# Four convolution blocks moved behind a residual norm with other row buffers, and 16 feed-forward blocks in the mixer

## The chip, the cores and the metric

The kernel runs on one core of a Trainium2 chip. The metric is the device time in microseconds. A core has a matrix engine (TensorE, PE in the profile; PEld are its weight loads), a vector engine (VectorE, DVE), an activation engine (ScalarE, ACT), GpSimd (POOL) and an engine that here only issues transfers (SyncE, SP). They run side by side, each through its own list of instructions in order, and wait for each other on semaphores.

## The reference

One layer over 1024 tokens of 1024 channels, float32. After an input norm, a combined projection feeds two groups of channels: 512 channels of RWKV-7 time mixing (a recurrence over tokens, 8 heads of 64) and 512 channels of a gated causal convolution with 31 taps, a layer norm and a silu. Both go through one output projection `w_out`, then a norm and a residual sum, then a gated feed-forward network whose inner activations pass a causal convolution of 3 taps.

```python
c = u[..., :D_CONV] * jax.nn.sigmoid(u[..., D_CONV:])
c = _causal_dwconv(c, cconv_w, cconv_b)          # 31 taps
c = jax.nn.silu(_layer_norm(c, cln_g, cln_b))
...
x1 = x + rms_norm(concat(rwkv_out, c) @ w_out)   # residual norm behind the mixer
f  = causal_conv3(rms_norm(x1) @ ffn_up)         # 2 x 2816 columns
out = x1 + rms_norm((gelu(f[:, :2816]) * f[:, 2816:]) @ ffn_down)
```

(The last three lines are shortened to what they compute.)

## The kernel before

The tokens are worked on in two halves of 512, and the recurrence in four quarters of 256 with four chunks of 64 tokens each. Every float32 matmul is made of three, with weights and activations split into a high and a low part: `wh` and `wl` of a weight (a cast on ScalarE, a subtraction on GpSimd, line 154), `f` and `h` pairs of activations.

The convolution of one half is four blocks of 128 channels, `conv(h, i)`. A block is one ScalarE instruction that starts an accumulator in the single PSUM bank "pc" and 30 VectorE instructions on it (line 393), the last of which writes the tile "co". `conv_norm(h)` then does the layer norm of the four blocks through transposes on TensorE, and its silu writes the tiles "co" again, which `w_out(h)` reads beside the recurrence's output "mixr".

`norm_ffn(0)` is the residual norm between the first half's w_out and its feed-forward part. For each of four row blocks of 128 tokens it loads x, loads two pieces of w_out's result from DRAM (`mixd`) into tiles "pt", adds them (line 838), squares the sum on ScalarE (line 839), and writes the row to DRAM (`x1d`). The rows are then scaled and transposed by TensorE with a diagonal matrix (line 846), and `channels` splits the result into the pairs "f" (lines 257 and 259), which are the input of the feed-forward blocks. Its last VectorE instruction is kept in `self.mark_lo`. The tiles "pt" are six, four of which hold results of the recurrence at that time.

A feed-forward block (`ffn_pair`) has two products of 24 matmuls with 512 columns; ScalarE starts the sum from the bank "pb", of which there are two (line 863), VectorE adds two taps (line 868), ScalarE does the gelu and VectorE multiplies the two (line 875). Of the first half's 22 blocks the mixer holds EARLY; their results stay in row tiles for the first KEPT, and the others go to DRAM as `early` and are read back when the feed-forward phase begins, after `w_out(1)`.

The order is made when the kernel is built. A list scheduler takes, for each engine, the ready instruction of the best stream: first, the recurrence ("rwkv", 1000), "top" (the first half's residual norm), "norm", "conv", "proj" (projections and feed-forward blocks), a smaller number being better; weight splits and the copies out of banks go ahead of their stream. With `issue_after` a step is not placed before a named instruction. `W[3].mark` is the last step of the inverses of quarter 3; `sts[0]["normed"]` is the last silu of `conv_norm(0)`.

Of the kernel before, what the change touches and what calls it, by code (L numbers as in the profile page):

```python
# [16 lines left out]
AF = mybir.ActivationFunctionType  # L17
ALU = mybir.AluOpType
# [4 lines left out]
P = 128  # L23
# [3 lines left out]
HALF = 512  # L27
# [19 lines left out]
BUFS = {"v": 2, "gd": 1, "pt": 6, "kk": 1, "l8": 5, "ca": 6, "ck": 6, "r": 2,  # L47
        "mixr": 1, "co": 4, "po": 1, "c": 4, "t2": 2}

EARLY, KEPT, EVERY = 12, 8, 2  # L50

PRIO = {"first": -1000, "top": 100000, "rwkv": 1000, "norm": 200000, "conv": 300000, "proj": 400000}

# [25 lines left out]
def constants():  # L79
    c = np.zeros((P, NCONST), np.float32)  # L80

    def put(name, v):
        c[:, COFF[name][0]:COFF[name][1]] = v

    i = np.arange(P)
    put("ident", np.eye(P))
    put("blk", (i[:, None] // 64) == (i[None, :] // 64))
    put("mask", (i[:, None] % CH) <= np.arange(-1, CH)[None, :])
    put("scan", (np.arange(QUARTER) % CH != 0)[None, :])
    return c  # L90


class Trunk:
# [714 lines left out]
    def row(self, tag, n):  # L808
        return (self.rowp if tag == "row" else self.nrowp).tile([P, D], F32, tag=tag, bufs=n, name=self.nm(tag))

    def norm_ffn(self, h, row, piece, hs, ahead=2, tags=("pn",), dg=None):


        nc = self.nc
        rows, diags = [], []
        cut = lambda c: slice(c * 512, (c + 1) * 512)

        def channels(tp):
            if not tp:
                hs.extend(self.pairs("f"))  # L820
            ts = slice(2 * tp, 2 * tp + 2)
            self.channels(rows[ts], "pre_ffn", hs, slice(tp * 256, (tp + 1) * 256), tags, diags[ts] or None)

        r = self.small.tile([P, 8], F32, tag="nr", bufs=1, name=self.nm("nr"))
        sf = self.small.tile([P, 4, 4], F32, tag="sf", bufs=1, name=self.nm("sf"))
        nc.vector.tensor_reduce(r[:, 0:4], self.ssq[:, 4 * h:4 * h + 4], AX.X, ALU.add)
        self.rstd(r[:, 4:8], r[:, 0:4], 1.0 / D, RMS_EPS)
        for t in range(4):
            if t == ahead:
                channels(0)  # L830
            tt = 4 * h + t
            rs = slice(tt * P, (tt + 1) * P)
            x, s = row(), sf[:, t]
            nc.sync.dma_start(x, self.a["x"][rs])
            for c in range(2):
                m = piece()
                nc.sync.dma_start(m, self.mixd[rs, cut(c)])
                nc.vector.scalar_tensor_tensor(x[:, cut(c)], m, r[:, 4 + t:5 + t], x[:, cut(c)], ALU.mult, ALU.add)
                nc.scalar.activation(m, x[:, cut(c)], AF.Square, accum_out=s[:, c:c + 1])
            nc.sync.dma_start(self.x1d[rs], x)  # L840
            nc.vector.tensor_tensor(s[:, 2:3], s[:, 0:1], s[:, 1:2], ALU.add)
            self.rstd(s[:, 3:4], s[:, 2:3], 1.0 / D, RMS_EPS)
            if dg is None:
                nc.scalar.activation(x, x, AF.Copy, scale=s[:, 3:4])
            else:
                nc.vector.tensor_scalar(dg[:, t], self.con("ident"), s[:, 3:4], None, ALU.mult)
                diags.append(dg[:, t])
            rows.append((x[:, :512], x[:, 512:]))
            yield
        channels(1)  # L850

# [101 lines left out]
    def run(self):  # L953
        self.setup()
        sts = [{}, {}]
        with ExitStack() as ctx:
            self.setup_mixer(ctx)
            h0, early = self.mixer(sts)
        with ExitStack() as ctx:
            self.setup_ffn(ctx)  # L960
            h1 = []
            norm = self.norm_ffn(1, lambda: self.row("nrow", 4),
                                 lambda: self.f2p.tile([P, HALF], F32, tag="f2", name=self.nm("m")), h1, 3)
            acts = self.ffn_up(0, h0, islice(norm, 3), EVERY, early)
            list(norm)
            outs = []
            self.ffn_down(0, acts, lambda *a: outs.append(a))
            acts = self.ffn_up(1, h1, (self.ffn_out(*a) for a in outs), 2)
            self.ffn_down(1, acts, self.ffn_out)

    def mixer(self, sts):
        nc, tc = self.nc, self.tc
        W = [None] * 4
# [32 lines left out]
        def step(fn, q, *args):  # L1006
            if q < 4:
                with self.stream("rwkv"):
                    fn(W[q], *args)
# [31 lines left out]
        def conv(h, i, behind=None):  # L1041

            with ExitStack() as gate, self.stream("conv"):
                if behind is not None:
                    gate.enter_context(tc.issue_after(behind.ins))
                self.conv(sts[h], i)
# [9 lines left out]
        cut = lambda t: (t[:, :512], t[:, 512:])  # L1056
        with self.stream("norm"):
            two = [self.tl("l8", [P, 2, D]) for _ in range(2)]
            rows = [cut(two[t // 2][:, t % 2]) for t in range(4)]
# [10 lines left out]
        with self.stream("norm"):  # L1070
            two = self.tl("mixr", [P, 2, D])
            rows = [cut(two[:, t]) for t in range(2)]
# [21 lines left out]
        prepare(2)  # L1094
        project(1, hs, "v0 v1 g")
        step(self.bonus, 2)
        conv(1, 0, sts[0]["normed"])
        conv(1, 1, sts[0]["normed"])
        with self.stream("proj"):
            self.w_out(0, mixes[0], [sts[0]["co", i] for i in range(4)])  # L1100
        mixes[1] = self.tl("mixr", [P, 4, HALF])
# [1 line left out]
        with self.stream("top"):  # L1103
            h0 = []
            dg = self.tl("kk", [P, 4, QUARTER]).rearrange("p a (b t) -> p (a b) t", b=2)
            list(self.norm_ffn(0, lambda: self.row("row", 4), lambda: self.tl("pt", [P, HALF]), h0, 2,
                               ("pb",), dg))
        conv(1, 2, W[3].mark)
        conv(1, 3)
        conv_norm(1)  # L1110
        early = []
# [16 lines left out]
def pack(ins):  # L1128
# [33 lines left out]
    def pad(v):  # L1162
# [15 lines left out]
    out["params"] = np.ascontiguousarray(  # L1178
        np.concatenate([vals[n].reshape(c, P) for n, c in PARAMS]).T)
    out["consts"] = constants()  # L1180
    out["post_mix"] = f("norm_post_mix")
    out["post_ffn"] = f("norm_post_ffn")
# [16 lines left out]
```

## Time and profile before

| | us |
|---|---|
| three runs, median | 1335.6 |
| lowest and highest | 1334.03, 1339.08 |
| profiled execution, own time | 1338.86 |
| its span | 1336.9 |
| TensorE busy | 1287.3 |
| VectorE busy | 761.1 |
| ScalarE busy | 668.1 |
| GpSimd busy | 574.6 |

Times inside the program are microseconds from the start of the span. In the groups of instructions, a line has the code line, the engine, the operation, what it writes and reads, the shapes and the count, then the busy time and the mean of one in ns, and behind the bar the idle time of the engine ahead of them with what ended it. In a table by stretch the columns are named in its head; PEclk is the clock granted to TensorE, 1.00 being 2.4 GHz. The busy time of a group of matmuls counts overlaps of groups twice.

### The profile page before, as it was taken

Reading aid. Unit: us, or ns where it says so; the run is one execution under the profiler, and the core shown is the slowest. Engines: PE = TensorE matmul, PEld = TensorE weight load, DVE = VectorE, ACT = ScalarE, POOL = GpSimd, SP = SyncE. Lnnn points to the kernel's source line nnn. Section 1 sums busy time; section 2 is a strip of 40 time slices with the busy share of each in tenths; the row PEclk is TensorE's granted clock in tenths of the full one; section 3 lists DMA queues with packets and bytes.
Section 4 is the critical chain, followed back from the end, with each engine's and each line's share of the span. In section 5 each row is a group of like instructions: output and inputs, shape, how many; then the busy total and the mean of one; then the engine's idle time right before and its main releaser. Section 6 shows DMA issues by size and latency. Waiting matters only on the chain.

```text
span 1336.9 us, 22830 instructions
## 1 busy us (share of the span) xinstructions
PE 1287.3 (96%) x8712; PEld 1044.5 (78%) x8712; DVE 761.1 (57%) x1342; ACT 668.1 (50%) x1324; POOL 574.6 (43%) x496
## 2 busy tenths in 40 slices
PE   6999989999899889999999999999999999999997
PEld 5777767777679867787799888888888888888886
DVE  5377998997799979894521645400046644441002
ACT  6563654657745764657543655522244444442222
POOL 4443423344333422454462545444454544454453
PEclk9999989999999999999999999999999999999999
DMA  6322211121123441222354543533334533333333
GB/s 213 82 75 62 73 40 49 49 72 54 50 68 103 136 158 42 72 61 82 103 161 142 189 142 111 181 95 95 95 111 143 154 106 95 98 100 95 95 95 111
DMA packets 73405, 135.60 MB, mean 101 GB/s; under 512 B 7920, under 2 KB 14448, under 8 KB 73296
## 3 DMA queue, kind: packets, MB, share of 16 engines
q1 hardware_dynamic: 73296, 134.14, 33.6%
q8 instruction: 69, 1.13, 0.4%
q14 instruction: 40, 0.33, 0.1%
HBM read 120.48 MB, written 13.63 MB: 100 GB/s over the span
## 4 chain that ended last, share of the span: by engine, by line
PE 78%; DVE 13%; ACT 4%; issue 3%; POOL 1%; DMA 1%; SPq 0%; POOLq 0%; DVEq 0%; ACTq 0%
PE pb L127 68%; PE pe L127 4%; DVE pc L393 4%; PE xs L127 3%; POOL wl L154 1%; DVE dw L570 1%; PE pe L142 1%; DVE sub L568 1%; ACT wh L154 1%; DVE h L259 1%; DVE pt L462 1%; DMA pt<-mixd 0%; DVE kk L463 0%; DVE m L154 0%; PE pc L142 0%
## 5 line engine op out<-in xcount | busy, mean ns | idle before, releaser
L154 POOL TENSOR_TENSOR wl<-wr,wh 128x512 fp32r<-128x512 f32 x360 | 474.8, 1320 | 600.2 <-ACT wh L154 573.2
L127 PE MATMUL pb<-f,wh 128*128 128x512 f32 x1408 | 438.4, 392 | 2.4 <-ACT pb L765 1.8
L154 ACT CAST wh<-wr 128x512 fp32r<-128x512 f32 x360 | 221.5, 616 | 431.3 <-PE pb L127 251.1
L127 PEld LDWEIGHTS pb<-f,wh 128*128 128x128 f32 x1408 | 264.0, 189 | 57.8 <-ACT pb L765 2.0
L127 PE MATMUL pb<-f,wl 128*128 128x512 f32 x704 | 277.2, 394 | 0.9 <-POOL wl L154 0.9
L127 PE MATMUL pb<-h,wh 128*128 128x512 f32 (+3 forms) x720 | 230.4, 400 | 2.0 <-ACT wh L154 1.4
L393 DVE SCALAR_TENSOR_TENSOR pc<-c,params,pc 128x512 f32<-128x512 f32 x232 | 174.1, 750 | 4.6 <-ACT pc L390 0.5
L868 DVE SCALAR_TENSOR_TENSOR acc<-pb,params,acc 128x511 f32<-128x511 f32 (+1 forms) x128 | 95.5, 746 | 138.7 <-ACT acc L863 98.0
L127 PEld LDWEIGHTS pb<-h,wh 128*128 128x128 f32 (+2 forms) x720 | 132.4, 189 | 34.3 <-ACT wh L154 3.4
L127 PEld LDWEIGHTS pb<-f,wl 128*128 128x128 f32 x704 | 132.7, 188 | 30.6 <-POOL wl L154 2.9
L127 PE MATMUL pb<-h,wl 128*128 128x512 f32 (+3 forms) x360 | 146.8, 408 | 2.8 <-POOL wl L154 2.7
L927 DVE TENSOR_TENSOR row<-pb,post_ffn 128x512 f32<-128x512 f32 x16 | 10.2, 685 | 209.2 <-ACT junk L926 209.2
L127 PE MATMUL pb<-wl,ahi 128*128 128x512 f32 x320 | 126.6, 396 | 0.0
L127 PE MATMUL pb<-wh,alo 128*128 128x512 f32 x320 | 126.4, 395 | 0.0
L127 PE MATMUL pb<-wh,ahi 128*128 128x512 f32 x320 | 88.5, 396 | 0.0
L127 PEld LDWEIGHTS pb<-h,wl 128*128 128x128 f32 (+2 forms) x360 | 67.9, 189 | 22.1 <-POOL wl L154 5.3
L127 PEld LDWEIGHTS pb<-wl,ahi 128*128 128x128 f32 x320 | 60.1, 188 | 14.6
L127 PEld LDWEIGHTS pb<-wh,alo 128*128 128x128 f32 x320 | 60.1, 188 | 14.4
L127 PEld LDWEIGHTS pb<-wh,ahi 128*128 128x128 f32 x320 | 59.7, 188 | 14.5
L868 DVE SCALAR_TENSOR_TENSOR pt<-pb,params,pt 128x511 f32<-128x511 f32 (+1 forms) x48 | 35.8, 745 | 33.5 <-ACT ecarry L865 33.1
L863 ACT ACTIVATE acc<-pb,params 128x512 f32<-128x512 f32 x64 | 49.6, 775 | 0.0
L154 DVE TENSOR_TENSOR alo<-acc,ahi 128x512 fp32r<-128x512 f32 x36 | 33.8, 945 | 22.2 <-ACT ahi L154 22.2
(268 smaller groups left out, 1785.7 us busy)
## 6 DMA issues: line engine op xcount, KB each, us to landing
wr<-ffn_up SPq DMA_DIRECT2D x176, 256.0 KB, 2.6
wr<-ffn_down SPq DMA_DIRECT2D x88, 256.0 KB, 2.6
wr<-w_in SPq DMA_DIRECT2D x80, 256.0 KB, 2.6
wr<-w_out SPq DMA_DIRECT2D x32, 256.0 KB, 2.7
mixd<-t SPq DMA_DIRECT2D x16, 256.0 KB, 3.4
nrow<-x1d SPq DMA_DIRECT2D x8, 512.0 KB, 4.2
out<-nrow SPq DMA_DIRECT2D x16, 256.0 KB, 2.4
l<-x SPq DMA_DIRECT2D x8, 256.0 KB, 5.6
```

The costliest lines, as they stand in the source:

```text
L127: return self.nc.tensor.matmul(out, lhsT, rhs, start=start, stop=stop, skip_group_check=skip)
L142: self.nc.tensor.transpose(out, in_, self.con("ident")[:n, :n])
L154: return self.nc.scalar.copy(hi, src), eng.tensor_tensor(lo, src, hi.bitcast(F32), ALU.subtract)
L259: self.mark_lo = nc.vector.scalar_tensor_tensor(lo[:, toks], pv, g, hi[:, toks].bitcast(F32), ALU.mult, ALU.subtract)
L393: nc.vector.scalar_tensor_tensor(out, c[:, j:j + HALF], w(j), acc, ALU.mult, ALU.add)
L462: nc.vector.tensor_tensor_scan(sg[:, l], self.con("scan"), sg[:, l], 0.0, ALU.mult, ALU.add)
L568: nc.vector.tensor_tensor(tv, dv[:, j + 1:, j:j + 1].broadcast_to([P, n, j]), dv[:, j:j + 1, :j].broadcast_to([P, n, j]), ALU.mult)
L570: nc.vector.tensor_tensor(dv[:, j + 1:, :j], dv[:, j + 1:, :j], tv, ALU.add)
L863: nc.scalar.activation(acc, ps, AF.Identity, scale=w(2), bias=self.par("fb", ch))
L868: nc.vector.scalar_tensor_tensor(acc[:, o:], ps[:, :HALF - o], w(j), acc[:, o:], ALU.mult, ALU.add)
L927: nc.vector.tensor_tensor(f[:, cs], ps, self.post_ffn[:, cs], ALU.mult)
```

## The change

All four blocks of the second half's convolution are built after `norm_ffn(0)`; the first is issued after `self.mark_lo`, and the others follow it through the bank "pc". Before, the first two were issued after `conv_norm(0)` and the other two after `W[3].mark`. The four row blocks of `norm_ffn(0)` live in two "row" tiles, a pair of "co" tiles and a pair of "t2" tiles, where they had four "row" tiles; x is loaded and x1d written in halves of 256 KB, in the second half's norm too. EARLY is 16 in place of 12, so eight blocks go through DRAM where four did.

```diff
-EARLY, KEPT, EVERY = 12, 8, 2
+EARLY, KEPT, EVERY = 16, 8, 2
+def cut2(t):
+    return t[:, :512], t[:, 512:]
...
-            nc.sync.dma_start(x, self.a["x"][rs])
+            for c in range(2):
+                nc.sync.dma_start(x[c], self.a["x"][rs, cut(c)])
             for c in range(2):
                 m = piece()
                 nc.sync.dma_start(m, self.mixd[rs, cut(c)])
-                nc.vector.scalar_tensor_tensor(x[:, cut(c)], m, r[:, 4 + t:5 + t], x[:, cut(c)], ALU.mult, ALU.add)
-                nc.scalar.activation(m, x[:, cut(c)], AF.Square, accum_out=s[:, c:c + 1])
-            nc.sync.dma_start(self.x1d[rs], x)
+                nc.vector.scalar_tensor_tensor(x[c], m, r[:, 4 + t:5 + t], x[c], ALU.mult, ALU.add)
+                nc.scalar.activation(m, x[c], AF.Square, accum_out=s[:, c:c + 1])
+                nc.sync.dma_start(self.x1d[rs, cut(c)], x[c])
...
-                nc.scalar.activation(x, x, AF.Copy, scale=s[:, 3:4])
+                for c in range(2):
+                    nc.scalar.activation(x[c], x[c], AF.Copy, scale=s[:, 3:4])
...
-        conv(1, 0, sts[0]["normed"])
-        conv(1, 1, sts[0]["normed"])
         with self.stream("proj"):
             self.w_out(0, mixes[0], [sts[0]["co", i] for i in range(4)])
...
-            list(self.norm_ffn(0, lambda: self.row("row", 4), lambda: self.tl("pt", [P, HALF]), h0, 2,
-                               ("pb",), dg))
-        conv(1, 2, W[3].mark)
+            homes = iter(['row', 'row', 'co', 't2'])
+
+            def row():
+                n = next(homes)
+                return cut2(self.row(n, 4)) if n == "row" else tuple(self.tl(n, [P, HALF]) for _ in range(2))
+
+            list(self.norm_ffn(0, row, lambda: self.tl("pt", [P, HALF]), h0, 2, ("pb",), dg))
+        conv(1, 0, self.mark_lo)
+        conv(1, 1)
+        conv(1, 2)
         conv(1, 3)
         conv_norm(1)
```

The change moves lines: line 393 of the kernel before is line 397 after, 568 and 570 are 572 and 574, 868 is 874, 875 is 881, 890 is 896, 834 is 839, 838 is 843.

VectorE in the inverses of quarter 2 (`sub` and `dw`), before: the first convolution block of the second half (line 393) stands between their steps.

```order
448 L568 TENSOR_TENSOR sub_3965<-dw 128x14
449 L393 SCALAR_TENSOR_TENSOR pc_4564<-c_3301,params,pc_4564 128x512
450 L570 TENSOR_TENSOR dw<-dw,sub_3965 128x14
451 L393 SCALAR_TENSOR_TENSOR pc_4564<-c_3301,params,pc_4564 128x512
452 L568 TENSOR_TENSOR sub_3968<-dw 128x26
453 L723 TENSOR_TENSOR mixr_1958<-mixr_1958,gn_3898 128x4x128
454 L393 SCALAR_TENSOR_TENSOR pc_4564<-c_3301,params,pc_4564 128x512
455 L570 TENSOR_TENSOR dw<-dw,sub_3968 128x13x2
456 L393 SCALAR_TENSOR_TENSOR pc_4564<-c_3301,params,pc_4564 128x512
457 L568 TENSOR_TENSOR sub_3971<-dw 128x36
```

The same place after:

```order
448 L572 TENSOR_TENSOR sub_3971<-dw 128x36
449 L727 TENSOR_TENSOR mixr_1958<-mixr_1958,gn_3898 128x4x128
450 L574 TENSOR_TENSOR dw<-dw,sub_3971 128x12x3
451 L572 TENSOR_TENSOR sub_3974<-dw 128x44
452 L574 TENSOR_TENSOR dw<-dw,sub_3974 128x11x4
453 L572 TENSOR_TENSOR sub_3977<-dw 128x50
454 L574 TENSOR_TENSOR dw<-dw,sub_3977 128x10x5
455 L572 TENSOR_TENSOR sub_3980<-dw 128x54
```

The convolution steps are gone from between the steps of the inverse.

VectorE in the residual norm of the first half, before: the additions of the third and fourth row block (`row<-pt,nr,row`, line 838), the scores (`l` and `ca`, lines 517, 518 and 526) and the first splits `f` between them.

```order
599 L838 SCALAR_TENSOR_TENSOR row_5977<-pt_5983,nr_5887,row_5977 128x512
600 L517 TENSOR_TENSOR l_792_5254<-pe_5287,const 128x4x64
601 L518 TENSOR_TENSOR ca_5285<-pe_5287,const 128x4x64
602 L702 TENSOR_TENSOR r_5467<-xs_94,XG_5479 64x256
603 L838 SCALAR_TENSOR_TENSOR row_5993<-pt_5995,nr_5887,row_5993 128x512
604 L259 SCALAR_TENSOR_TENSOR f_5926<-pb_5941,params,f_5925 128x256
605 L259 SCALAR_TENSOR_TENSOR f_5928<-pb_5941,params,f_5927 128x256
606 L841 TENSOR_TENSOR sf_5888<-sf_5888 128x1
607 L526 TENSOR_TENSOR l_639_4014<-l_639_4014,gd_4235 128x1024
```

After, at the second and third row block (the third is in "co" tiles):

```order
580 L843 SCALAR_TENSOR_TENSOR row_5845<-pt_5853,nr_5821,row_5845 128x512
581 L574 TENSOR_TENSOR dw<-dw,sub_5374 128x5x10
582 L572 TENSOR_TENSOR sub_5377<-dw 128x44
583 L574 TENSOR_TENSOR dw<-dw,sub_5377 128x4x11
584 L846 TENSOR_TENSOR sf_5822<-sf_5822 128x1
585 L572 TENSOR_TENSOR sub_5380<-dw 128x36
586 L152 TENSOR_SCALAR var_5859<-sf_5822 128x1
587 L574 TENSOR_TENSOR dw<-dw,sub_5380 128x3x12
588 L572 TENSOR_TENSOR sub_5383<-dw 128x26
```

The scores have moved ahead of the norm, and steps of the inverses of quarter 3 stand between the additions.

SyncE where the feed-forward phase begins, before: the last pieces of w_out(1) are written, the blocks kept in DRAM come back, then rows of x and the first weights.

```order
231 L767 DMA mixd<-t_1214_8067 128x2x256
232 L890 DMA acc_8126<-early 128x512
233 L890 DMA acc_8132<-early 128x512
234 L890 DMA acc_8138<-early 128x512
235 L890 DMA acc_8144<-early 128x512
236 L834 DMA nrow_8336<-x 128x1024
237 L834 DMA nrow_8532<-x 128x1024
238 L834 DMA nrow_8728<-x 128x1024
239 L834 DMA nrow_9156<-x 128x1024
240 L160 DMA wr_8259<-ffn_up 128x512
```

After, the end of the same stretch:

```order
270 L164 DMA wr_8665<-ffn_up 128x512
271 L839 DMA nrow_9187<-x 128x512
272 L896 DMA acc_8520<-early 128x512
273 L896 DMA acc_8526<-early 128x512
274 L164 DMA wr_8683<-ffn_up 128x512
```

Six blocks come back ahead of these rows, and the last two stand between the weights.

## Rows read from the trace of the kernel before

**Rows 1.** The head of the page: the span, then the busy time, share and count of TensorE and its weight loads and of the other engines.

```profile
span 1336.9 us, 22830 instructions
...
PE 1287.3 (96%) x8712; PEld 1044.5 (78%) x8712; DVE 761.1 (57%) x1342; ACT 668.1 (50%) x1324; POOL 574.6 (43%) x496
```

**Rows 2.** The table by stretch: from and to, its length, busy time and count of PE, PEld, DVE, ACT and POOL, then the granted clock, the share of the DMA engines and GB/s.

```profile
368.60:397.50 28.90, 26.58 (x135) 20.97 (x134) 28.61 (x54) 13.48 (x25) 11.95 (x11) 0.96 0.25 71
397.50:463.60 66.10, 63.11 (x851) 58.59 (x849) 63.39 (x103) 42.81 (x97) 25.20 (x20) 0.99 0.37 107
463.60:510.20 46.60, 38.08 (x454) 28.64 (x453) 38.95 (x95) 29.27 (x77) 9.84 (x14) 0.90 0.42 134
510.20:626.00 115.80, 115.75 (x1150) 92.44 (x1151) 96.55 (x157) 66.05 (x139) 49.93 (x42) 0.99 0.23 65
...
727.60:732.00 4.40, 2.60 (x8) 1.91 (x7) 1.28 (x2) 2.67 (x9) 0.00 (x0) 0.77 0.42 135
732.00:861.00 129.00, 128.92 (x580) 106.08 (x579) 69.97 (x102) 73.38 (x149) 63.42 (x50) 0.99 0.49 156
```

**Rows 3.** The waits of TensorE: what waited, for whom, the time in total, how often, the longest. The first is of 368.6 to 397.5, the second of 397.5 to 463.6, the third of 463.6 to 510.2, the last two of 510.2 to 646.

```profile
PE pe L142 <- DVE mixr L737: 2.1, 1, 2.1
...
PE pb L127 <- POOL wl L154: 1.8, 2, 0.9
...
PE pb L127 <- DVE sub L568: 2.0, 1, 2.0
...
PE pc L142 <- DVE t L409: 1.3, 1, 1.3
PE pb L127 <- POOL wl L154: 0.6, 1, 0.6
```

**Rows 4.** Groups of VectorE from 368.6 to 463.6.

```profile
L393 DVE SCALAR_TENSOR_TENSOR pc<-c,params,pc 128x512 f32<-128x512 f32 x58 | 43.4, 748 | 0.6
```

**Rows 5.** Groups of TensorE's matmuls, the first three from 463.6 to 510.2 (scores, broadcasts of 512 columns, chunk products), the last from 510.2 to 626 (small steps of the inverses).

```profile
L127 PE MATMUL pe<-l,l 64*128 64x128 f32 x64 | 6.5, 290 | 0.9 <-DVE ca L518 0.6 <-DVE sf L841 0.4
L127 PE MATMUL pe<-pt,const 128*128 128x512 f32 x8 | 6.0, 866 | 0.1
L127 PE MATMUL Y<-r,l 64*64 64x64 f32 x48 | 4.6, 250 | 0.0
...
L127 PE MATMUL pe<-l,dw 32*16 32x16 f32 (+1 forms) x192 | 4.5, 178 | 0.0
```

**Rows 6.** The timeline of the gap: start, duration, engine, line, what was done, and in brackets the idle time ahead with what ended it. First VectorE (additions, the diagonal), then ScalarE (the last Square), then TensorE.

```profile
474.63 1.41 DVE L838 SCALAR_TENSOR_TENSOR row<-pt,nr,row 128x512 f32<-128x512 f32 x2
...
489.02 1.17 DVE L838 SCALAR_TENSOR_TENSOR row<-pt,nr,row 128x512 f32<-128x512 f32 x1
...
495.53 0.74 DVE L838 SCALAR_TENSOR_TENSOR row<-pt,nr,row 128x512 f32<-128x512 f32 x1
...
499.51 0.64 ACT L839 ACTIVATE pt<-row 128x512 f32<-128x512 f32 x1
...
507.14 1.42 PE L127 MATMUL pb<-kk,row 128*128 128x128 f32 x9 [2.02 <-DVE sub L568]
...
510.25 1.19 PE L127 MATMUL pb<-f,wh 128*128 128x512 f32 x2 [0.20 <-DVE sub L568]
```

**Rows 7.** The table by stretch again, where the granted clock falls; the columns as in rows 2.

```profile
463.60:467.10 3.50, 1.56 (x53) 1.25 (x53) 3.47 (x6) 2.82 (x10) 1.43 (x2) 1.00 0.87 183
...
467.10:473.90 6.80, 6.75 (x50) 3.51 (x49) 1.73 (x5) 3.05 (x10) 1.52 (x2) 0.50 0.85 274
508.10:511.50 3.40, 3.21 (x13) 2.74 (x12) 2.36 (x9) 1.68 (x4) 0.00 (x0) 0.50 0.01 2
```

**Rows 8.** Groups of VectorE beside the feed-forward blocks, the first three from 517.7 to 598.6 (convolution, gate, product), the others from 510.2 to 646 (group norm, low split).

```profile
L393 DVE SCALAR_TENSOR_TENSOR pc<-c,params,pc 128x512 f32<-128x512 f32 x58 | 43.6, 751 | 1.2 <-ACT pc L390 0.2
L868 DVE SCALAR_TENSOR_TENSOR pt<-pb,params,pt 128x511 f32<-128x511 f32 (+1 forms) x20 | 14.9, 743 | 1.6 <-ACT ecarry L865 1.6
L875 DVE TENSOR_TENSOR row<-pt,pt 128x512 f32<-128x512 f32 x5 | 4.5, 904 | 0.0
...
L723 DVE TENSOR_TENSOR mixr<-mixr,gn 128x512 f32<-128x512 f32 x4 | 5.7, 1424 | 0.3 <-POOL gn L149 0.3
L154 DVE TENSOR_TENSOR l<-mixr,l 128x512 fp32r<-128x512 f32 x4 | 4.2, 1118 | 4.2 <-ACT l L154 4.2
```

**Rows 9.** The timeline there: ScalarE takes up a product and VectorE ends it; then the end of the fourth convolution block and a product of the gate.

```profile
580.99 0.78 ACT L863 ACTIVATE pt<-pb,params 128x512 f32<-128x512 f32 x1
...
585.65 0.73 DVE L868 SCALAR_TENSOR_TENSOR pt<-pb,params,pt 128x510 f32<-128x510 f32 x1
...
591.81 0.73 DVE L393 SCALAR_TENSOR_TENSOR co<-c,params,pc 128x512 f32<-128x512 f32 x1
592.46 1.79 DVE L875 TENSOR_TENSOR row<-pt,pt 128x512 f32<-128x512 f32 x1
```

**Rows 10.** TensorE's timeline: the last transposes of the convolution's norm; the last feed-forward matmuls ahead of w_out(1), and its first.

```profile
642.82 0.63 PE L142 MATMUL pc<-const,t 128*128 128x128 f32 x4 [1.28 <-DVE t L409]
...
680.18 0.62 PE L127 MATMUL pb<-f,wh 128*128 128x512 f32 x2
...
681.55 1.12 PE L127 MATMUL pb<-wm,l 128*128 128x256 f32 x8
```

**Rows 11.** SyncE's timeline where the feed-forward phase begins.

```profile
730.73 1.76 SPq L890 DMA_DIRECT2D acc<-early  x4
```

More of the change, by code (lines that the diff above doesn't have):

```diff
@@ L847, in norm_ffn @@
                 diags.append(dg[:, t])
-            rows.append((x[:, :512], x[:, 512:]))
+            rows.append(x)
             yield
@@ L961, in run @@
             h1 = []
-            norm = self.norm_ffn(1, lambda: self.row("nrow", 4),
+            norm = self.norm_ffn(1, lambda: cut2(self.row("nrow", 4)),
                                  lambda: self.f2p.tile([P, HALF], F32, tag="f2", name=self.nm("m")), h1, 3)
```

## The prediction

> **What bounds the kernel now.** I read the head of the page first: TensorE is busy 1287.3 of the span's 1336.9 us [rows 1]. So an edit can only pay where TensorE stands still or runs at half clock, and I looked for those places with the table by stretch [rows 2]. From 732 us on nothing is left to win (128.92 of 129.00 us busy up to 861). Ahead of the first feed-forward matmul, at 510.25, three stretches lose something: the half's projections up to 397.5 (2.3 us idle, the difference of its length and its busy time), w_out of the first half (3.0 us) and the stretch from its end to 510.2, which I call the gap (8.5 us idle, at a granted clock of 0.90). The waits of TensorE say for whom [rows 3]: 2.1 us for VectorE's mixr, 1.8 us for weight splits of GpSimd, and in the gap many short ones. VectorE is the cause of the first: it is busy 28.61 of 28.90 and 63.39 of 66.10 us there [rows 2], and 58 instructions of the convolution at 748 ns, 43.4 us, are mixed into the chunk inverses [rows 4]. These are what the change takes away from there.
>
> **Part 1, projections and w_out(0).** The convolution steps leave VectorE between 368.6 and 463.6, so what else it does there ends up to 43 us earlier. The stretch up to 397.5 can give 2.3 us of idle time and 1.1 us that the clock of 0.96 costs in 28.9 us; most of it is the wait for mixr, which should go. I take 3 us (0 to 3.4), and w_out(0) starts at 394.5 in place of 397.5. In w_out(0) TensorE's order has 114 more matmuls than before (32 score products, 49 chunk products, two broadcasts of 512 columns, 31 small ones). Each stands for two records of the trace, so by the forms' rows [rows 5] a score is 0.20 us, a chunk product 0.19, a broadcast 1.5 and a small step 0.05: 6.5 + 9.3 + 3.0 + 1.6, some 20 us as groups; but the groups of the gap add up to 49 us where TensorE was busy 38, since matmuls overlap, and part of it ran at half clock. I take 14 us (12 to 17). That is work brought forward, no loss. Of the 3.0 us idle 2 go; the wait for weight splits stays. Gain 2, between 0 and 3. It ends at 394.5 + 66.1 + 14 - 2 = 472.6.
>
> **Part 2, the gap.** What sets its length is the chain of the residual norm, four row blocks one after the other [rows 6]. Only two "pt" tiles are free for the pieces of mixd, so each row block waits for a round trip: the first piece of row 1 is added at 474.63 and that of row 4 at 489.02, 4.8 us a row. To that come delays: the first addition stands behind a wait of VectorE for TensorE, 2.3 us after the norm's statistics were there; the last addition came at 495.53, some 5 us after its piece could have been used, behind other work on VectorE; its Square began at 499.51, 3.2 us after it, behind ScalarE's key copies; and TensorE waited 2.0 us for an inverse's step just before the first feed-forward matmul. These make 12.6 us, so the gap lies between 34 us (46.6 less all of them) and 46.6. In the new order the scores and key copies are over before the gap, but the inverses of quarter 3, 14 pairs of short steps, now stand between the additions, and two additions of "pt" that wait for TensorE stand behind the first pair. The round trip stays, since the change gives more row buffers and no more pieces. I take 40 us, the middle, and the first feed-forward matmul at 512.6. What the gap holds of TensorE's work falls: 32 scores, 49 chunk products and two broadcasts go, 160 small steps come; 18.8 us of groups against 8, and with the same overlap and clock some 5 to 9 us, I take 6. So of the 6.6 us by which the gap is shorter 6 were moved ahead: gain 0.6, between -5 and +7.
>
> The clock: after 1.56 busy of 3.50 us, from 463.6, the granted clock falls to 0.50, that is 1.2 GHz, and stays there to 473.9; at 508.1 it falls again [rows 7]. The Trainium skill says in "TensorE: Matmul & The Clock Gate", section "HAM oscillation — how this bites in real kernels", that waits between bursts of matmuls put the engine back to half clock, so that the next burst starts cold. The rows agree. A gap with less work in it would, by that rule, also lie at half clock at its end, which would add about 1 us to the first feed-forward block (3.4 us at half clock instead of the 1.25 us of it that lie behind 510.25); without the rule nothing changes in the sum.
>
> **Part 3, feed-forward beside convolution.** All 120 convolution steps now run from the first feed-forward block on, where 60 ran before. VectorE's order from there to the end of the fourth block: 120 x 751 ns = 90.1 us; 48 gate steps at 743 = 35.7; 12 products at 904 = 10.8; four each of the group norm and the lower split, 5.7 and 4.2 [rows 8]; 35 short ones, about 16. Sum 162 us. Neighbours that don't depend on each other start 0.08 us before the end of the one ahead (591.81 + 0.73 against 592.46 [rows 9]); some 150 such pairs make it 151 us. TensorE has 576 feed-forward matmuls until then, at 0.228 us each (six in 680.18 to 681.55 [rows 10]) 131 us, and 236 small ones, 17 to 25: 148 to 156 us. VectorE begins 3 us behind, with the first product, so at the end it is 2 behind (151 + 3 - 152). A product's bank was given back 5.4 us after ScalarE had taken it up (580.99 to 585.65 + 0.73 [rows 9]) in a stretch where TensorE stood still for 0.05 of 115.80 us [rows 2]. So no stop on balance: 0, between -1.9 (the waits of 1.3 us for the convolution's norm and of 0.6 for weights [rows 3] go too) and +14 (below).
>
> **Part 4, the rest.** Four more feed-forward blocks come before w_out(1) and four fewer after it: no change of TensorE's work. Between the norm of the convolution (its last transposes at 642.82) and w_out(1) (681.55 now [rows 10]) only 23 matmuls are left as cover, 5.2 us, where there were 38 us; a silu, the splits of "co" and the weights' casts must fit in: 0 to +3. After w_out(1) eight "early" blocks come back where four did; their four issues began at 730.73 [rows 11]. The last two reloads need a buffer that must first come free, and weights stand behind them on SyncE: 0 to +4. The stretch already loses 1.8 us of 4.4 [rows 2]. I take +0.5 for both. GpSimd's and ScalarE's work are the same in sum, and the rows written in halves, 256 KB, only let the first half land earlier: nothing.
>
> **Sum**, against the profiled execution's own 1338.86 us: -3 -2 -0.6 +0 +0.5 = -5.1, so 1333.8. That execution lies 3.3 us above the median of 1335.6. So 1330.5, I say 1330.
>
> **Rivals.** A: VectorE becomes the bound of the feed-forward stretch. Without the overlap of neighbours it needs 162 + 3 us against 148 of TensorE; less the 5.4 us of slack it stops TensorE for 12 us, and w_out(1) then also waits for the convolution's norm. It decides when VectorE really needs over about 155 us. For it: VectorE was busy 96.55 of 115.80 us [rows 2] with half of the steps; one product took 1.79 us (592.46 [rows 9]) where the five took 0.90 in the mean. Against it: before, it kept up with the same mix. The Trainium skill, "SBUF — State Buffer", section "SBUF: two separate sides", says that a VectorE instruction with two SBUF operands is held up by a GpSimd instruction that has the port pair they share. The trace agrees for the 1.79 us, while convolution steps, with one operand from PSUM, keep 751 ns beside busy GpSimd; by the rule the price falls on the 12 products and the splits alone, some 3 us. A gives 1330 + 12 = 1342, 1340 to 1346.
>
> B: the norm runs through at its round trips, 34 us, the rest of the idle time ahead goes (3.4 + 3.0 - 5 = 1.4 us) and so do the 1.9 us of waits in part 3: 6 + 1.4 + 1.9 better than the forecast, 1321. For it: scores and copies are out of its way. Against it: short inverse steps stand in every pair of additions.
>
> C: the idle time only moves. The chunk products fill w_out, the gap keeps 46.6 us and has less to fill it: 6.6 us back, 1337, no change. For it: the last wait ahead of the feed-forward blocks [rows 6] is for an inverse of the recurrence, not for the norm.
>
> **Chances.** Forecast 0.45 (its own range 1325 to 1336), A 0.20, B 0.20, C 0.15. The range 1319 to 1344 holds B's and most of A's. A difference under 0.5%, 6.7 us, can't be told from none: faster is below 1328.9, slower above 1342.3. B and four in ten of the forecast make faster 0.38; half of A and what I have not seen make slower 0.17; the same is 0.45.
>
> **What would show it.** The first matmul of w_out(0) near 394.5, its last near 473; the first feed-forward matmul near 513; between there and the end of the convolution no wait of TensorE for VectorE's gate steps. Long waits for a bank there mean A; a gap of 35 us B; one of 46 C. The forecast is wrong altogether if w_out(1) begins over 10 us after its last feed-forward matmul.

## The result and the profile after

The changed kernel takes 1340.2 us in the median of 19 executions (1337.0 to 1347.4), the kernel before 1335.8 us beside it. The ratio of the means is 1.0046, 95% interval 1.0028 to 1.0063: slower by some 6 us in the mean and 4.4 in the median, where a gain of 5 was forecast. The interval leaves no room for a gain.

The 19 times are no one heap. Ten lie at 1337.0 to 1340.2 and nine at 1342.8 to 1347.4. In all executions of the changed order in this study (this kernel, and three that differ from it in buffers or reloads only, 66 in all) none lies between 1340.3 and 1342.2: 40 are below, with a mean granted clock of 0.980 to 0.988, and 26 above, at 0.974 to 0.983 (18 of them under 0.980). I call them the lower and the upper group; their means here are 1338.3 and 1345.9 us. The profile below is of an execution of the lower group, 1337.5 us. That it is shorter than the profile of before (1338.9) is therefore no sign of a gain.

The table by stretch of the changed kernel, with the columns of [rows 2]. The first stretch ends at the first matmul of w_out(0), the second at its last, the third (the gap) at the first feed-forward matmul.

```profile
368.60:392.10 23.50, 21.57 (x113) 16.79 (x112) 20.76 (x46) 12.94 (x24) 10.30 (x10) 1.00 0.23 64
392.10:474.20 82.10, 79.56 (x1077) 71.61 (x1075) 47.78 (x78) 46.74 (x109) 26.08 (x24) 0.98 0.33 102
474.20:515.90 41.70, 31.65 (x575) 26.37 (x573) 30.97 (x81) 27.32 (x69) 7.74 (x12) 0.84 0.39 130
515.90:680.00 164.10, 163.33 (x1054) 130.91 (x1051) 152.84 (x226) 84.06 (x176) 75.23 (x59) 1.00 0.30 88
```

VectorE is no longer full ahead of w_out(0) and beside it (20.76 of 23.50 and 47.78 of 82.10 us, where [rows 2] have 28.61 of 28.90 and 63.39 of 66.10), as the change intends. It is nearly full beside the feed-forward blocks, 152.84 of 164.10, and TensorE doesn't suffer from that: 163.33 us busy. The gap is shorter, 41.7 for 46.6 us, at a clock of 0.84 for 0.90.

The waits of TensorE in the same kernel, as in [rows 3]: the first up to 392, the next three in the gap, the last two from 516 to 680.

```profile
PE pe L146 <- DVE mixr L727: 1.9, 1, 1.9
...
PE pb L131 <- DVE sf L846: 2.4, 1, 2.4
PE pe L131 <- issue: 1.7, 1, 1.7
PE xs L131 <- ACT r L696: 1.3, 1, 1.3
...
PE pb L131 <- DVE pt L874: 0.3, 1, 0.3
PE pb L131 <- POOL wl L158: 0.3, 1, 0.3
```

The wait for mixr that was to go with the convolution (2.1 us in [rows 3]) is still there with 1.9. For VectorE's gate steps TensorE waits 0.3 us in all.

The gap's timeline, as in [rows 6], and the end of the convolution's norm, as in [rows 10]:

```profile
481.58 1.21 DVE L843 SCALAR_TENSOR_TENSOR row<-pt,nr,row 128x512 f32<-128x512 f32 x1
...
498.80 0.74 DVE L843 SCALAR_TENSOR_TENSOR t<-pt,nr,t 128x512 f32<-128x512 f32 x1
...
502.18 0.75 DVE L843 SCALAR_TENSOR_TENSOR t<-pt,nr,t 128x512 f32<-128x512 f32 x1
...
515.90 0.73 PE L131 MATMUL pb<-f,wh 128*128 128x512 f32 x2
...
715.52 0.60 PE L146 MATMUL pc<-const,t 128*128 128x128 f32 x4
...
721.00 0.88 PE L131 MATMUL pb<-wm,l 128*128 128x256 f32 x6
```

The first piece of the fourth row block is added 17.2 us after that of the first (before 14.4), its second piece follows 3.4 us later (before 6.5). The last transposes of the norm come at 715.52, without a wait, and w_out(1) follows its last feed-forward matmul at 721.00.

### The profile page after: what moved, and what is told of

Its sections match the earlier page's. It is cut to its first block, busy times and chain, and to the rows that moved or that the text cites. A ratio compares the mean times of both kernels' runs of the same rounds, so it can differ in the third digit from the quotient of the medians.

```text
span 1335.4 us, 22890 instructions
## 1 busy us (share of the span) xinstructions
PE 1284.2 (96%) x8712; PEld 1044.5 (78%) x8712; DVE 763.5 (57%) x1342; ACT 669.9 (50%) x1330; POOL 574.3 (43%) x496
## 5 line engine op out<-in xcount | busy, mean ns | idle before, releaser
L874 DVE SCALAR_TENSOR_TENSOR acc<-pb,params,acc 128x511 f32<-128x511 f32 x112 | 83.4, 745 | 116.9 <-ACT acc L869 98.0
L933 DVE TENSOR_TENSOR row<-pb,post_ffn 128x512 f32<-128x512 f32 x16 | 10.2, 685 | 206.3 <-ACT junk L932 206.3
L131 PEld LDWEIGHTS pb<-wh,alo 128*128 128x128 f32 x320 | 60.1, 188 | 14.4
L874 DVE SCALAR_TENSOR_TENSOR pt<-pb,params,pt 128x511 f32<-128x511 f32 x64 | 47.7, 745 | 14.0 <-ACT ecarry L871 13.4
L869 ACT ACTIVATE acc<-pb,params 128x512 f32<-128x512 f32 x56 | 43.4, 774 | 0.0
```

The source lines that it names most:

```text
L131: return self.nc.tensor.matmul(out, lhsT, rhs, start=start, stop=stop, skip_group_check=skip)
L869: nc.scalar.activation(acc, ps, AF.Identity, scale=w(2), bias=self.par("fb", ch))
L874: nc.vector.scalar_tensor_tensor(acc[:, o:], ps[:, :HALF - o], w(j), acc[:, o:], ALU.mult, ALU.add)
L933: nc.vector.tensor_tensor(f[:, cs], ps, self.post_ffn[:, cs], ALU.mult)
```

## The experiments

**The same kernel again.** No edit.

> The changed kernel once more, for the spread of its times and another profile. Its runs lie in two groups, ten at 1337 to 1340 us and nine at 1343 to 1347, and the profile read so far (1337.5) is of the lower one. Theory K (clock): the upper group has TensorE at 1.2 GHz for some 16 us more, so its mean granted clock is near 0.977 where the lower has 0.980 to 0.988; this would be around or behind the gap between w_out(0) and the first feed-forward block, which holds less matmul work now. Theory E (early blocks): the upper group comes from the feed-forward phase's start, where eight blocks come back from DRAM, and the clock is only a sign of it. Both: median 1338 to 1344.

Measured: 1338.8 us median of 11 executions, ratio 1.0015 (1.0004 to 1.0026); eight in the lower group, three in the upper (1342.3 to 1344.6). The profile fell on the lowest of the upper, 1342.3 us. A later profile (the version with eight buffers, below) fell on 1347.2 us. Of that one, the table by stretch where the feed-forward blocks begin, at 523.3:

```profile
505.00:510.00 5.00, 4.23 (x135) 3.96 (x134) 3.29 (x11) 2.91 (x8) 1.10 (x2) 0.78 0.26 96
510.00:515.00 5.00, 3.53 (x21) 3.49 (x22) 0.65 (x2) 1.99 (x4) 0.00 (x0) 0.56 0.02 3
515.00:520.00 5.00, 5.00 (x58) 4.46 (x57) 1.42 (x4) 2.66 (x6) 0.00 (x0) 0.50 0.00 0
520.00:525.00 5.00, 5.00 (x50) 4.36 (x48) 2.54 (x6) 3.02 (x8) 0.00 (x0) 0.50 0.01 3
525.00:530.00 5.00, 5.00 (x19) 3.69 (x19) 4.79 (x7) 0.93 (x2) 1.14 (x1) 0.73 0.00 0
```

and of the changed kernel in the lower group:

```profile
505.00:510.00 5.00, 3.27 (x98) 3.13 (x91) 1.73 (x5) 2.09 (x5) 0.00 (x0) 0.76 0.03 7
510.00:515.00 5.00, 5.00 (x74) 4.67 (x73) 2.26 (x6) 3.93 (x9) 0.00 (x0) 0.90 0.00 0
515.00:520.00 5.00, 5.00 (x52) 4.15 (x51) 4.00 (x7) 3.43 (x7) 0.58 (x1) 1.00 0.02 3
520.00:525.00 5.00, 5.00 (x63) 3.62 (x62) 3.96 (x6) 2.30 (x6) 1.64 (x3) 1.00 0.20 52
525.00:530.00 5.00, 5.00 (x79) 4.07 (x78) 4.45 (x7) 3.88 (x8) 2.26 (x2) 1.00 0.30 84
```

In both the clock falls between 507 and 511, among small matmuls and the transposes of the norm. In the lower group it is back at 511.0, after 3.4 us, ahead of the first feed-forward matmul; in the upper TensorE is busy without a pause from 515 on and is still at 1.2 GHz until 527.7, 17.1 us after the fall. In the profile of 1342.3 us the stretch is from 509.6 to 523.3, 13.7 us, all of it busy, the last 4 us with feed-forward matmuls. First that stretch, then that of the changed kernel in the lower group:

```profile
509.60:523.30 13.70, 13.70 (x116) 11.95 (x115) 6.50 (x13) 7.09 (x16) 0.00 (x0) 0.50 0.01 2
...
507.60:511.00 3.40, 3.22 (x20) 3.19 (x21) 0.02 (x1) 2.00 (x4) 0.00 (x0) 0.50 0.02 5
```

The other two profiles of the lower group have 3.4 us there too.

So the stretch at half clock is 10 and 14 us longer in the two profiles of the upper group, worth 5 to 7 us of matmuls. Gap and blocks together, up to w_out(1), are 4.0 and 5.6 us longer in them than the mean of the three lower profiles (251.0 and 252.6 for 247.0). The groups' means are 7.6 us apart for the changed kernel and 4.6 in these runs. So most of the distance is the clock at the end of the gap, as theory K had it, but not all: the profile of 1347.2 us reaches w_out(0) 2.6 us later than the mean of the lower ones. What decides in which of the two ways an execution goes is not known.

**EARLY 12 in the changed kernel, and the late convolution alone in the kernel before.**

```diff
-EARLY, KEPT, EVERY = 16, 8, 2
+EARLY, KEPT, EVERY = 12, 8, 2
```

and, in the kernel before:

```diff
-        conv(1, 0, sts[0]["normed"])
-        conv(1, 1, sts[0]["normed"])
...
-        conv(1, 2, W[3].mark)
-        conv(1, 3)
+        conv(1, 0, self.mark_lo)
+        conv(1, 1)
+        conv(1, 2)
+        conv(1, 3)
```

> The changed kernel with EARLY 12: convolution late and other row buffers stay, four blocks fewer in the mixer and four reloads fewer. Theory K: the two groups stay, median 1338 to 1343. Theory E: the second group goes, and the 2.2 us that the feed-forward phase lost in the profile come back: 1331 to 1335.

> The kernel before with all four convolution blocks behind the last split of the first half's residual norm, EARLY 12 and four row tiles as before. Theory K: like the changed kernel, two groups, median 1338 to 1343. Theory E: the gain of 5 us ahead of w_out(0) without the loss: 1330 to 1334. With only 12 blocks beside it the convolution ends nearer to w_out(1); if VectorE paces that, w_out(1) waits up to 10 us and it is 1340 to 1346 under both.

Measured: 1358.7 us (ratio 1.0151, 1.0135 to 1.0167) and 1352.9 us (1.0129, 1.0108 to 1.0149), both above all that was expected; the last sentence of the second expectation named the place, at about half its price. With 12 blocks the convolution's norm falls into w_out(1). TensorE's waits from 683 to 750 in the changed kernel with EARLY 12, and the stretch in which they lie:

```profile
PE pc L146 <- DVE t L413: 5.6, 2, 2.8
PE pc L146 <- ACT co L418: 3.3, 2, 1.7
PE pb L131 <- ACT l L158: 2.1, 1, 2.1
```

```profile
705.00:725.00 20.00, 9.92 (x54) 8.54 (x55) 6.19 (x12) 5.80 (x15) 1.77 (x3) 0.66 0.03 13
```

TensorE stands still for half of these 20 us, at a mean clock of 0.66. From its first matmul to its last, w_out(1) takes 66.1 and 66.2 us in these two profiles, 52.4 with EARLY 14 and 47.0 in the changed kernel. So the four blocks more are what makes the late convolution possible: they are its cover, worth 13 to 15 us between the lower groups. Both kernels have two groups of times again (1351.5 to 1353.7 and 1358.1 to 1360.9), and the two profiles, both of upper ones, have 1.2 GHz from 510 to 527. Theory E, by which the second group would go with the reloads, is out.

**EARLY 16 alone, twice.**

```diff
-EARLY, KEPT, EVERY = 12, 8, 2
+EARLY, KEPT, EVERY = 16, 8, 2
```

> The kernel before with EARLY 16 alone: eight blocks go through DRAM, the convolution and the rows as before. Theory K: as before, 1334 to 1338. Theory E: 1338 to 1343, some of its runs 8 us above the others.

> The kernel before with EARLY 16 once more, as the twin on the same chip: 0.3% over the kernel before in one group, as in its first five runs (1340.2 to 1343.4 at clocks of 0.985 to 0.988); no times with a mean clock under 0.982 under theory K, since its gap is that of the kernel before.

Measured: 1342.0 (ratio 1.0032, 1.0020 to 1.0044) and 1340.5 us (1.0023, 1.0011 to 1.0036): four blocks more cost 3 to 4 us by themselves. One group, with clocks of 0.982 to 0.989 (and one execution at 1346.3, at 0.984). From the end of w_out(1) on, the first profile has this on SyncE and on TensorE:

```profile
775.93 3.64 SPq L890 DMA_DIRECT2D acc<-early  x6
779.61 1.52 SPq L834 DMA_DIRECT2D nrow<-x  x3
781.23 0.68 SPq L160 DMA_DIRECT2D wr<-ffn_up  x1
781.96 0.85 SPq L834 DMA_DIRECT2D nrow<-x  x1
783.84 0.33 SPq L160 DMA_DIRECT2D wr<-ffn_up  x1
785.59 2.12 SPq L890 DMA_DIRECT2D acc<-early  x2
787.79 11.97 SPq L160 DMA_DIRECT2D wr<-ffn_up  x5
```

```profile
PE pb L127 <- ACT pb L765: 1.8, 1, 1.8
PE pb L127 <- ACT wh L154: 1.5, 2, 0.9
```

The first wait is there before the change too. The second, for weights, is new against the profile of before. Behind it the second half's residual norm has fewer feed-forward blocks to hide in, 6 for 10, and TensorE waits some 0.85 us for weights 14 us after the first ffn_down matmul, in the changed kernel too, where the profile of before has no wait.

The stages show where the price lies. The four blocks lengthen the stretch from the first feed-forward matmul to w_out(1) by 43.4 us (171.3 in the profile of before, a mean of 214.7 in four with EARLY 16 and its order). From the last matmul of w_out(1) to the end, where the four blocks are missing, the four take 567.8 to 569.3 us and the kernel before 609.2, which is 39.9 to 41.4 less. So 2 to 3.5 us are lost behind w_out(1). TensorE's idle time there is 8.6 us before and 10.1 to 11.7 in the four, and their waits for weights add up to 1.5 to 3.2 us.

**Eight buffers for the reloads, in both.**

```diff
-        self.f2p = pool("f2p", 6)
+        self.f2p = pool("f2p", 8)
```

> The changed kernel with eight buffers for the reloads and the feed-forward sums (f2p) in place of six, so that the last two reloads need not wait for one and the weights behind them on SyncE start earlier. Theory R (part of what EARLY 16 costs is this queue): 1 to 2 us less in both groups, 1336 to 1338 and 1342 to 1346, and the waits for weights of 0.6 us some 20 us after w_out(1) are gone. Rival: no change in the groups; the cost is the amount of reloads and not the wait for buffers.

> The kernel before with EARLY 16 and eight such buffers. With six it took 1342.0 against 1337.3 of the kernel before, and its profile has waits of 1.8 us for weights 17 us after w_out(1) and of 1.0 us later. Theory R: 1339 to 1340.5 (in runs where the kernel before has 1337), the 1.8 us gone. Rival: 1341.5 to 1343.

Measured: 1339.4 (1.0028, 1.0013 to 1.0044; eight below, four above) and 1340.2 us (1.0028, 1.0017 to 1.0040). The groups of the first are where they were. The second is 1.9 us under its twin in the median, with the kernel before 0.8 lower in those runs; its ratio is inside the twin's interval, and its profile still has three waits for weights, 2.3 us together. The wait for a buffer isn't the cause, as far as these runs can tell.

**The reloads in two lots**, four of them after two feed-forward blocks, in both.

```diff
-        for i, e in enumerate(early):
...
-        for i in range(len(early), FT):
+        order = list(range(KEPT + 4)) + [n, n + 1] + list(range(KEPT + 4, n)) + list(range(n + 2, FT))
+        for i in order:
```

> The kernel before with EARLY 16, where the feed-forward phase reads back four blocks as the kernel before does, then works on two feed-forward blocks, and reads back the other four after that. The same blocks are spilled and read. Theory Q (the 0.3% that EARLY 16 costs are the weights that stand behind eight reloads and the rows on SyncE's queue): the waits of 1.8 us for weights 17 us after w_out(1) go and it is 2 to 3 us under its twin with eight reloads at once: 1339 to 1340 where the kernel before has 1337. Rival V: it is the volume of spills and reloads or the work on them, wherever they stand: no difference to the twin, within 1 us.

> The changed kernel with its reloads in two lots in the same way. Theory Q: both groups fall by 1 to 2 us, the lower to 1336 to 1338, about the kernel before, and the upper to 1342 to 1346; theory V: both as they are, 1337.5 to 1340 and 1342 to 1347. Theory K under both: two groups, since nothing ahead of w_out(1) differs; in the upper the mean clock is 0.974 to 0.982.

Measured: 1340.0 (1.0015, 1.0003 to 1.0027) beside 1340.5 for the twin, and 1339.7 us (1.0030, 1.0015 to 1.0046; eight below, four above). The waits for weights of the first are 0.7 us where the twin in the same runs had 2.3:

```profile
PE pb L127 <- ACT pb L765: 1.8, 1, 1.8
PE pb L127 <- POOL wl L154: 0.7, 1, 0.7
```

so the queue is part of it, but the medians differ by 0.5 us only. Theory Q named 2 to 3 and is not borne out; in the changed kernel there is nothing. The wait of 0.85 us behind the first ffn_down matmul is in this version too. So the price is mostly waits for weights behind w_out(1), in two places, and what makes the weights late there is shown in part only: the kernel with three late blocks and EARLY 12, below, has 1.2 us of such waits with no reload more than before.

**The row buffers as before**, with the late convolution and EARLY 16 (the two diffs above together).

> The kernel before with all four convolution blocks late and EARLY 16, but the rows of the residual norm in four row tiles and x in 512 KB as before. It differs from the changed kernel by the row buffers and halves alone. If these do nothing: two groups as there, median 1338 to 1344. If the row tiles hold up the first feed-forward blocks, whose results need them: 2 to 6 us more than the changed kernel.

Measured: 1341.9 us (1.0055, 1.0036 to 1.0074): six at 1338.3 to 1339.7 and six at 1344.0 to 1348.0. These are the groups of the changed kernel. The other row buffers and the halves of 256 KB neither cost nor bring anything that these runs can show.

**EARLY 14 in the changed kernel.**

> The changed kernel with EARLY 14. Its convolution ends in the same place, but there are two feed-forward blocks (22 us) fewer to cover it. From EARLY 12 (1358.7) and 16 (1339 to 1340): if the wait of w_out(1) for the convolution is all of the 19 us, two blocks remove it in full or nearly, and two reloads fewer save 1 us: 1338 to 1345. If not: about the middle, 1349.

Measured: 1341.5 us (1.0056, 1.0034 to 1.0078), five at 1340.6 to 1342.0, two at 1346.7 and 1350.0. So of the cover that the four blocks give, the first two bring 12 us (1353 to 1341 in the lower groups) and the last two 2 to 3. The profile, of the last one, has 1.2 GHz from 510 to 527.

**One convolution block more behind the norm, three in all, EARLY 12**, in the kernel before.

```diff
-        conv(1, 1, sts[0]["normed"])
...
-        conv(1, 2, W[3].mark)
+        conv(1, 1, self.mark_lo)
+        conv(1, 2)
```

> The kernel before with one convolution block more behind the first half's residual norm (three there, one between the inverses as before), EARLY 12, other things as before. No reloads are added, so what EARLY 16 costs alone (4.3 us) is saved; half of what the convolution's leaving brings ahead of w_out(0) (4 us in the profiles) remains: 2 us. Its order keeps 37 matmuls, 8 us, between the last norm of the convolution and w_out(1). Theory K with its two groups in part: 1334 to 1341. If VectorE is then what w_out(1) waits for: 1340 to 1348.

Measured: 1335.9 us, ratio 0.9999 (0.9986 to 1.0013), no upper group by the clock (0.985 to 0.991). No reloads more, no fall of the clock at the end of the gap in its profile (the granted clock is 1.00 from 487 to the first feed-forward matmul at 512.1), and no gain. It is the best of the versions with a later convolution, and it can't be told from the kernel before. The upper group came with all four blocks late, at EARLY 12, 14 and 16, and in no order with one or two of them early.

**TensorE kept busy in the gap.** Two versions of the changed kernel with transposes of a constant that nothing reads, in a stream behind all others: 112 from the last matmul of w_out(0) on, and 40 behind the second row block of the norm. The diff is of the first; the lines that name the stream and keep the last matmul are left out.

```diff
...
+        ps = self.bank("pc")
+        with tc.issue_after(self.last_mm.ins), self.stream("fill"):
+            for _ in range(28):
+                for j in range(4):
+                    self.transpose(ps[:, j * P:(j + 1) * P], self.con("ident"))
```

> The changed kernel with 112 transposes of a constant into the unused bank pc, in the lowest stream, issued from the last matmul of w_out(0) on: they stand where TensorE would wait between w_out(0) and the first feed-forward block, and nothing reads them. Theory K (the clock falls in the gap and in part of the executions stays at 1.2 GHz for some 14 us of the feed-forward blocks): the granted clock is 1.00 from 475 to 530 or nearly so, the upper group of times goes, and all runs lie at 1333 to 1338, below the lower group of the changed kernel (1337 to 1340). Rival W: the half clock in the gap is not what costs the time, since TensorE waits there anyway; the fill delays the chain by some us and the two groups stay: 1340 to 1350.

> The changed kernel with 40 transposes of a constant into the unused bank pc, all behind the residual norm's first two row blocks, so in the last third of the gap only; nothing reads them. In the executions of the upper group the clock fell to 1.2 GHz at 510 and came back at 524, in those of the lower group it was back at 511. Theory K: with TensorE kept busy ahead of 510 the fall at 510 is rarer or gone: few or no times above 1342, the lower group where it was, 1337 to 1341 (the fill may cost it 1 to 3 us). Rival W: the clock at 510 doesn't hang on the idle time in the last third: two groups as before, about half the times above 1342.

Measured: 1342.7 us (1.0056, 1.0038 to 1.0074), six executions at 1341.6 to 1346.6, clocks 0.982 to 0.989; and 1350.0 us (1.0098, 1.0084 to 1.0112), five at 1348.7 to 1351.8, 0.980 to 0.983. No mean clock is under 0.980 in either, and from 515 to 620 both profiles have 1.00. The times don't fall: the fill moves the first feed-forward matmul to 524.5 in the first, and in the second TensorE later waits 4.0 us for VectorE's gate steps, in another order of the blocks. Both times lie above what theory K expected. With 11 executions and one profile of each these two bear out K on the clock and say nothing of what a kernel without the loss would take. The first, in the gap of the changed kernel:

```profile
495.00:500.00 5.00, 4.58 (x161) 4.26 (x162) 4.11 (x8) 2.68 (x6) 0.96 (x2) 0.72 0.50 172
500.00:505.00 5.00, 5.00 (x154) 4.58 (x155) 2.01 (x5) 2.92 (x8) 1.61 (x3) 0.50 0.42 143
...
474.10:515.90 41.80, 40.36 (x666) 35.15 (x665) 28.96 (x75) 26.69 (x65) 8.50 (x13) 0.88 0.41 131
```

## Why the prediction was wrong

In the profile of the lower group every sign that the prediction had named for its forecast came or nearly came: w_out(0) from 392.1 to 474.2, the first feed-forward matmul at 515.9, 0.3 us of waits for gate steps, and w_out(1) straight behind its last feed-forward matmul. The time was wrong all the same. What failed is the sum: the term of +0.5 us for "the rest" (Part 4), which measured 3 to 4, the clock at the end of the gap, which the sum left out, and the 3 us of Part 1, which can't be seen. The measured median lies inside the range of 1319 to 1344 by luck: the range reached up there for rival A, which did not happen.

The stages are read from TensorE's first and last matmuls. For an order as in the kernel before up to the feed-forward blocks there are five profiles (the kernel before, EARLY 16 twice, with eight buffers, in two lots), for the changed order five too, three of the lower group (the changed kernel, the one with old rows, the one in two lots) and two of the upper.

| stage | forecast, us | before, mean | lower | upper |
|---|---|---|---|---|
| first matmul of w_out(0) | -3 | 394.6 (392.7 to 396.3) | 393.1 | 394.7 |
| w_out(0) | +12 | 68.8 | 81.8 | 81.8 |
| gap | -6.6 | 47.1 | 41.9 | 44.8 |
| feed-forward up to w_out(1), 16 blocks | -8 | 214.7 | 205.1 | 207.0 |

(The first matmul of w_out(0) is at 395.8 in the profile of before; from 397.5, which the prediction used, its matmuls follow each other. In the forecast the last row is the work brought forward, 14 less 6; the mean of before is over the four profiles that have 16 blocks.)

**Part 1's 3 us can't be seen.** They were taken from one execution. The same order reached w_out(0) at 392.7 to 396.3 in five, with different clock falls far ahead of it: at 186 to 202 the granted clock was 0.57 in the profile of before and 0.89 in that of the changed kernel, in a place that the change doesn't touch.

```profile
186.00:202.00 16.00, 12.86 (x45) 9.78 (x46) 15.82 (x25) 7.37 (x14) 0.61 (x3) 0.57 0.06 17
```

```profile
186.00:202.00 16.00, 12.27 (x83) 9.26 (x85) 15.79 (x26) 7.18 (x14) 1.49 (x2) 0.89 0.07 20
```

The five lie, by their own times, 1.6 us above the medians of their kernels, so the 0.9 us between all five and all five of the changed order (393.7) is not a gain that these can show. The earliest of each order, 392.7 and 392.1, are those with the least time at half clock ahead of it (6.8 and 10.2 us, the others 19 to 24). And the wait for mixr stayed at 1.9 us without the convolution steps, so they were not what held it up; what does was not looked into. That VectorE was 99% busy there was true, and it was no bound: most of what filled it was work of a lower stream.

**w_out(0) and the work brought forward** came out near to what was worked out: +13.0 for +12, -9.6 for -8. In the two profiles of before and after TensorE's busy time in w_out(0) grew by 14.7 us (64.8 to 79.6), where 14 was forecast, but of the 3.0 us of idle time there 2.5 stayed, where 1 was forecast. **The gap** is 5.2 us shorter in the lower group for the 6.6 forecast; the delays that I had counted went, and the waits for inverse steps and the half clock (0.84) took part of them back. Up to w_out(1) the sum is -1.5 + 13.0 - 5.2 - 9.6 = -3.3 us in the lower group for -5.6.

**Part 3 held.** Rival A, VectorE as the bound, is wrong: TensorE lost 0.77 of 164.10 us. The overlap of neighbours is what the forecast of 151 us of VectorE for 162 us of instructions rests on, and it was there: up to the last convolution step 160.3 us of instructions took 148.4 us. The trace agrees with the rule of the Trainium skill ("SBUF — State Buffer", "SBUF: two separate sides") that the prediction had cited, as far as it went: the convolution steps, with one operand in PSUM, kept 750 ns.

**Part 4 was mis-sized.** I had +0.5 us for reloads and cover, and four blocks moved for nothing. EARLY 16 alone measured 3.1 and 4.3 us: the stretch behind w_out(1) gives back 39.9 to 41.4 us for the 43.4 that the blocks cost ahead of it. The cover of 5.2 us ahead of w_out(1) sufficed for the convolution's norm; w_out(1) took 47.0 us for 46.2, with a wait of 0.5 us for a weight.

**The clock was known and priced too low.** The prediction had it as "about 1 us" of the first block, and its sum left it out. The upper group, 26 of 66 executions, lies some 7 us above the lower, 4 to 6 of them at the end of the gap in the two profiles; in the mean the 7 us are +3.

Together: -3.3 at most and nearer to -2 without Part 1's share, and +3 to +4 for EARLY 16, come near to the lower group's +2.1 (its mean over the median of before in the same runs, between 1.3 and 2.9 in the five sets of runs); the upper group lies some 7 higher. The median depends on how many executions fall in it. That these parts add up is worked out, not shown by one run; shown are the price of EARLY 16 (alone), that the late convolution needs it (1353 and 1359 without), that the row buffers do nothing that can be measured, and that the profiles of the upper group have the longer stretch at half clock.

## What to carry to other kernels

An engine that is full with work of a low stream is not a bound; look at what its high-stream instructions waited for before counting their room as gain. A stage that one profile shows should be held against the spread between executions of everything ahead of it: here the same order gave 3.6 us of difference at one matmul. And a move that needs another one to be covered (late convolution, more early blocks) has to earn that one's price too.

## What was not expected of the hardware

The clock fell to 1.2 GHz with TensorE busy for 40.36 of 41.80 us in the gap (the first fill), and stayed there from 497.2 to 507.5. Ahead of the fall, from 490 on, TensorE had run transposes, the fill's among them, products of 64 columns and 128 steps of 32 rows and 16 columns, with one wait of 1.26 us. The Trainium skill ("TensorE: Matmul & The Clock Gate", "HAM oscillation — how this bites in real kernels") tells of waits of several microseconds between bursts; this trace has none of that length there, so their absence did not keep the clock up here.

And once at 1.2 GHz, with TensorE busy, it stayed there for 13.7 us in one execution (509.6 to 523.3) and for 3.4 us in another of the same program (507.6 to 511.0), in nearly the same place of the same instructions: a kernel whose gap ends in such a place has two times, and one profile shows one of them.
